# Seven products for the second group's down projection of a hybrid decoder layer

## The chip, the core and the metric

The kernel runs on one core of a Trainium2 chip. The core has TensorE (PE, matrix products), VectorE (DVE), ScalarE (ACT), GpSimd (POOL) and SyncE (SP), which here only issues transfers. The metric is the time of one execution in microseconds on the device; a kernel's time is the median of several timed runs. One more execution is taken with the profiler.

## The reference

One decoder layer is computed in fp32 for 2048 prompt tokens (16 blocks of 128) and 32 sample tokens, model width 1024, hidden width 4096:

```python
def decoder_layer(x, p, lp, state):
    xn = rms_norm(x, lp['norm_mix_pre'])
    qk_raw, v_m, o_m, gates, q_a, k_a, v_a = split_projection(xn @ lp['w_in'])
    ...
    mix = jnp.concatenate([y_m, y_a], axis=-1) @ lp['w_out']
    x = x + rms_norm(mix, lp['norm_mix_post'])
    u = rms_norm(x, lp['norm_ffn_pre'])
    f = jnp.square(jax.nn.relu(u @ lp['w_up'])) @ lp['w_down']
    x = x + rms_norm(f, lp['norm_ffn_post'])
    x = x + jax.nn.sigmoid(x @ lp['w_pgate']) * (p @ lp['w_pproj'])
    return x, (c_new, n_new, m_new, conv_new, k_new, v_new)
```

`y_m` is an mLSTM with four heads (chunks of 128 tokens), `y_a` a sliding-window attention with eight heads, both from the one projection. The change touches the product with `w_down`.

## The kernel before, in words

The blocks form six chunks (3, 3, 3, 3, 2, 2 blocks) and three groups of two chunks. First the projection with both attentions runs over all chunks (0 to about 700 us). Then each group goes through the output projection ("mix"), the MLP and the gate. The second group, whose MLP runs from about 1530 to 1960 us, is group 1 (blocks 6 to 11); the first group's MLP runs from 850 to 1300 us.

Every fp32 product is three passes on numbers that are split into a high and a low part, high x high, high x low and low x high (`mm3`). A high part is a cast on ScalarE, a low part a subtraction on VectorE or GpSimd (`split`, `wsplit`; L230 and L231 for hidden activations, L253 and L254 for weights). Weights come through a ring of 7 pair tiles (high and low, 512 KB) and 5 raw tiles. At its first use a weight tile is loaded raw, split, and stored to memory by GpSimd's queue (L281); later it is loaded already split by SP's queue (`w<-wk`).

The MLP goes through the hidden width in 16 steps of 256. In a step `up_both` makes the hidden activations of both chunks, each as two tiles of 128 x 384, by a Strassen scheme: seven products of four inner blocks each instead of eight (steps 2 to 15). Its sums are adds on VectorE that read PSUM (L1732), each followed by relu and square on ScalarE (L1652, L1653), a cast (L230) and a low part (L231). `down` then multiplies the hidden tiles with `w_down` plainly: 2 chunks x 2 halves of 512 columns x 3 blocks x 2 tiles x 3 passes, 72 matmuls of 128 x 512 a step. Each block and half ends in a PSUM buffer (three of them) that VectorE adds into `f` (L1757).

What sets the order: TensorE's work is written in program order. A class `Flow` counts TensorE's modelled time, and lets side generators (attention, sums of activations) emit their instructions when their due time, given by the numbers that they yield, is reached. A scheduler orders the other engines, except for instructions that are pinned in program order (`here`).

## Time and profile before

| what | us |
|---|---|
| median of three timed runs | 2620.46 (2619.96 to 2620.51) |
| the profiled execution | 2614.14 |
| its span in the trace | 2612.0 |
| TensorE busy in the span | 2525.7 |
| VectorE busy | 1481.4 |
| ScalarE busy | 973.9 |
| GpSimd busy | 620.4 |

The mean granted TensorE clock was 0.993. Times in the trace are counted from the start of the span. In rows of groups the two numbers behind the bar are the busy time of the group and the mean of one in ns; in rows of the timeline the first two are start and duration in us. "w" is a split weight, "wr" and "wb" a raw one, "wk" its stored copy, "hh" and "hl" the high and low part of hidden activations, "re" their sums before the split, "up" and "dn" the products in PSUM.

### The profile page before, as it was taken

The numbers are of one execution on the slowest core, as the hardware profiler recorded it, in microseconds if no ns is written. First come the engines' busy times: TensorE is split into PE (matmuls) and PEld (weight loads), VectorE is DVE, ScalarE is ACT, GpSimd is POOL, SyncE is SP. The second block draws the span as 40 slices with busy tenths as digits, with TensorE's granted clock in tenths as the row PEclk, the third lists the DMA queues.
The fourth block names the chain that finished last, engine by engine and source line by source line (L and its number), as shares of the span: only waits on it lengthen the run. The fifth ranks groups of instructions, "written<-read, shape, count | busy, mean of one in ns | idle before, by whom it ended". The sixth has DMA issues, their size and how long they took to land.

```text
span 2612.0 us, 39335 instructions
## 1 busy us (share of the span) xinstructions
PE 2525.7 (97%) x14260; PEld 2198.5 (84%) x14260; DVE 1481.4 (57%) x3162; ACT 973.9 (37%) x2167; POOL 620.4 (24%) x988
## 2 busy tenths in 40 slices
PE   7999999999899999999999999999999999999998
PEld 7788878878688888888877789999998879999986
DVE  6676666665667656656744654444446346545553
ACT  5545444444445444444523442222223134222232
POOL 5311111112433666666523300000001011000010
PEclk9999999999999999999999999999999999999999
DMA  9755656576798666666799765555556899777786
GB/s 321 280 201 182 216 176 221 202 254 217 253 345 291 256 248 254 243 254 250 268 344 316 262 208 185 193 186 188 188 189 231 296 332 360 257 254 254 256 304 236
DMA packets 220433, 651.10 MB, mean 249 GB/s; under 512 B 25397, under 2 KB 59401, under 8 KB 220224
## 3 DMA queue, kind: packets, MB, share of 16 engines
q1 hardware_dynamic: 170032, 474.02, 53.1%
q0 software_dynamic: 50160, 174.54, 17.3%
q8 instruction: 113, 1.85, 0.3%
q14 instruction: 80, 0.66, 0.1%
q10 hardware_dynamic: 48, 0.03, 0.0%
HBM read 494.34 MB, written 155.25 MB: 249 GB/s over the span
## 4 chain that ended last, share of the span: by engine, by line
PE 77%; DMA 8%; DVE 8%; issue 4%; ACT 3%; POOL 1%; SPq 0%; ACTq 0%; DVEq 0%; POOLq 0%
PE up L147 22%; PE dn L147 22%; PE pg L147 5%; PE mo L147 4%; PE v L147 3%; DMA w<-wk 3%; PE o L147 2%; DMA wk<-w 2%; PE qk L147 2%; PE gv L147 2%; DVE hl L231 1%; PE qa L147 1%; PE aT L151 1%; PE aO L147 1%; PE pv L147 1%
## 5 line engine op out<-in xcount | busy, mean ns | idle before, releaser
L147 PE MATMUL dn<-w,hh 128*128 128x512 f32 x1792 | 563.6, 396 | 7.2 <-ACT re L1652 4.2
L1757 DVE TENSOR_TENSOR f<-f,dn 128x512 f32<-128x512 f32 x420 | 287.2, 687 | 220.5 <-PE dn L147 218.4
L147 PEld LDWEIGHTS dn<-w,hh 128*128 128x128 f32 x1792 | 334.0, 189 | 85.5 <-DVE f L1757 7.0
L147 PE MATMUL dn<-w,hl 128*128 128x512 f32 x896 | 354.4, 396 | 1.6 <-DVE hl L231 1.6
L1732 DVE TENSOR_TENSOR re<-up,re 128x384 f32<-128x384 f32 (+1 forms) x294 | 152.0, 517 | 320.7 <-PE up L147 320.6
L147 PEld LDWEIGHTS dn<-w,hl 128*128 128x128 f32 x896 | 168.7, 188 | 43.3 <-DVE hl L231 5.2
L1733 ACT COPY re<-up 128x384 f32<-128x384 f32 (+1 forms) x42 | 18.8, 448 | 392.0 <-PE up L147 392.0
L1652 ACT ACTIVATE re<-re 128x384 f32<-128x384 f32 (+1 forms) x168 | 83.0, 494 | 206.7 <-DVE re L1732 203.2
L231 DVE TENSOR_TENSOR hl<-re,hh 128x384 fp32r<-128x384 f32 (+1 forms) x192 | 136.9, 713 | 16.1 <-ACT hh L230 15.1
L281 POOL DMA_DIRECT2D wk<-w x242 | 133.8, 556 | 30.0 <-DVE w L254 25.1
L253 ACT CAST w<-wr 128x512 fp32r<-128x512 f32 (+2 forms) x152 | 89.2, 597 | 94.6 <-PE up L147 31.1
L253 ACT CAST w<-wb 128x512 fp32r<-128x512 f32 x98 | 60.6, 620 | 168.5 <-PE dn L147 114.5
L254 POOL TENSOR_TENSOR w<-wr,w 128x512 fp32r<-128x512 f32 (+2 forms) x76 | 100.3, 1319 | 78.7 <-ACT w L253 77.7
L1459 POOL DMA_DIRECT2D x<-x1d x16 | 8.7, 545 | 463.5 <-PE up L147 449.4
L254 POOL TENSOR_TENSOR w<-wb,w 128x512 fp32r<-128x512 f32 x70 | 92.4, 1320 | 110.4 <-ACT w L253 110.0
L1653 ACT ACTIVATE re<-re 128x384 f32<-128x384 f32 (+1 forms) x192 | 94.9, 494 | 5.9
L230 ACT CAST hh<-re 128x384 fp32r<-128x384 f32 (+1 forms) x192 | 92.6, 482 | 8.3
L1066 ACT ACTIVATE s<-s,swt 128x257 f32<-128x257 f32 (+1 forms) x128 | 63.3, 496 | 66.1 <-DVE swt L1063 66.1
L1060 DVE CUSTOM_DVE_ANT_0 s<-aS,cst,sink 128x256 f32<-128x256 f32 (+1 forms) x128 | 57.1, 473 | 50.2 <-PE aS L147 49.8
L147 PE MATMUL up<-t2h,w 128*128 128x384 f32 (+1 forms) x336 | 85.2, 321 | 0.0
L147 PE MATMUL up<-t0h,w 128*128 128x384 f32 (+1 forms) x336 | 85.2, 320 | 0.0
L147 PE MATMUL up<-t1h,w 128*128 128x384 f32 (+1 forms) x336 | 85.1, 320 | 0.0
(1526 smaller groups left out, 6404.2 us busy)
## 6 DMA issues: line engine op xcount, KB each, us to landing
w<-wk SPq DMA_DIRECT2D x728, 512.0 KB, 4.7
wk<-w POOLq DMA_DIRECT2D x238, 512.0 KB, 7.5
wr<-in_w_down_dram SPq DMA_DIRECT2D x64, 256.0 KB, 8.2
wb<-in_w_up_dram SPq DMA_DIRECT2D x28, 512.0 KB, 6.8
w<-wk SPq DMA_DIRECT2D x20, 528.0 KB, 4.0
x<-in_x_prompt_dram SPq DMA_DIRECT2D x16, 512.0 KB, 4.6
y<-yd SPq DMA_DIRECT2D x32, 256.0 KB, 6.7
xr<-in_x_prompt_dram POOLq DMA_DIRECT2D x16, 512.0 KB, 8.6
```

Source lines behind the costliest of these rows:

```text
L147: ins = self.pe.matmul(out, lhsT, rhs, start=start, stop=stop)
L230: act.copy(hi, src)
L231: dve.tensor_tensor(lo, src, hi.bitcast(F32), ALU.subtract)
L253: act.copy(hi, src)
L254: ins = (eng or weng()).tensor_tensor(lo, src, hi.bitcast(F32), ALU.subtract)
L281: here(put(self.kept[key], t.bitcast(U32)))
L1060: dve.tensor_tensor_reduce(s_[:, s, lo : 2 * P], pS[:, s, lo:], bias[:, j, lo:], 1.0 if s == 0 else 0.0625, sink[:, h : h + 1], ALU.add, A ...
L1066: act.activation(e_, e_, AF.Exp, bias=nm[:, s : s + 1], accum_out=sm[:, s : s + 1])
L1652: act.activation(t, src, AF.Relu)
L1653: act.square(t, t)
L1732: add = lambda out, a, b: dve.tensor_tensor(out, a, b, ALU.add)
L1757: dve.tensor_tensor(out(i), out(i), ps, ALU.add)
```

## The change

In group 1, steps 2 to 13 (`SEVEN`, 12 steps) make the down product by seven products too. Two steps form a pair: `up_seven` makes the hidden tiles of each step and four more combinations of them (s1 to s4), and `down_seven`, after the odd step, runs seven products, each over the two steps in one PSUM buffer. A product is added into one or two halves of `f`, or into an accumulator U of three tiles, which `share` adds to three quarters of `f` after step 13. Of the sums, s1, t1 and t3 (the inputs of s2 and s4) and the low parts of s1, s2 and s4 are on GpSimd.

The right sides are three plain blocks of `w_down` a step and four differences of blocks. The differences are made in the projection: a new side generator, `differences`, starts with the second chunk. For each step it loads four blocks on GpSimd's queue into raw tiles of the ring, subtracts four times on GpSimd and stores four tiles (`td`). In the MLP they are loaded raw by SP's queue and split, cast on ScalarE and low part on GpSimd. The tile pools are shared out anew: the ring's `wide` pool is closed at step 2 in group 1, `sp2` has one buffer, the gain for the norm after the MLP is loaded behind `share` in this group. `MIXF` lets the preparation of the second chunk's mix in group 0 start later behind its loads (18 instead of 6).

```diff
--- before
+++ changed
...
 MIXW = 6.0
+MIXF = 18.0
 LODVE = 2
 STEPS = FF // (FS * P)
+SEVEN = range(2, STEPS - 2)
+SGROUP = 1
+DIFW = 10.0, 4.0, 10.0
...
             return self.get(key, n, make)
+        def diff(self, key, src):
+            def make(h, l):
+                raw = self.load(512)
+                dma(raw, src)
+                wsplit(h, l, raw, pool)
+            return self.get(key, 512, make)
...
             return ("u", s, q), lambda key: ring.multi(key, [(0, FS * P, rows)], 2, FS * P)
+        def diff(s, i):
+            return ("t", s, i), lambda key: ring.diff(key, td[s, i])
+        def rows_seven(steps):
+            for i, k, half in ((0, 0, 0), (3, 0, 0), (0, 1, 0), (1, 0, 0), (4, 0, 0), (0, 1, 1), (2, 0, 0)):
+                for s in steps:
+                    yield diff(s, i) if i else row(w_down, s * FS + k, half)
...
                     yield product(s, i)
-                yield from rows_down(s)
+                if gi == SGROUP and s in SEVEN:
+                    if s % 2:
+                        yield from rows_seven((s - 1, s))
+                else:
+                    yield from rows_down(s)
...
+    td = {(s, i): dram.tile([P, 512], F32, name=f"td{s}{i}") for s in SEVEN for i in range(1, 5)}
     ring.set_plan(plan())
+    def differences():
+        sub = lambda out, a, b: here(pool.tensor_tensor(out, a, b, ALU.subtract))
+        for s in SEVEN:
+            b11, b21, b12, b22 = b = [ring.load(512) for _ in range(4)]
+            for n, t in enumerate(b):
+                k = s * FS + n % 2
+                here(put(t, w_down[k * P : (k + 1) * P, n // 2 * 512 : n // 2 * 512 + 512]))
+            yield DIFW[0]
+            for i, out, x, y in ((1, b11, b12, b11), (3, b12, b22, b12), (2, b22, b22, b11), (4, b21, b21, b22)):
+                sub(out, x, y)
+                yield DIFW[1]
+            for i, out in ((1, b11), (3, b12), (2, b22), (4, b21)):
+                here(put(td[s, i], out))
+            yield DIFW[2]
...
     for ci, blocks in enumerate(CHUNKS):
+        if ci == 1:
+            prep.add(differences())
         project(ci, blocks)
     pe.drain(swa)
+    pe.drain(prep)
...
             todo.append((None, "s", load_y(lp, "ld", "s")))
-        yield MIXW
+        yield MIXF if (gi, ci) == (0, 1) else MIXW
...
     wp = es2.enter_context(tc.tile_pool(name="wp", bufs=WBUF, reuse_waits="tile"))
-    sp2 = es2.enter_context(tc.tile_pool(name="sp2", bufs=2, reuse_waits="tile"))
+    sp2 = es2.enter_context(tc.tile_pool(name="sp2", bufs=1, reuse_waits="tile"))
     open_lp()
     dec = pe.side()
     def mlp(gi, chunks, sample):
         nonlocal gffn
-        gffn = gain(A["norm_ffn_post"], f"gffn{gi}")
         G = f"{gi}"
+        if gi != SGROUP:
+            gffn = gain(A["norm_ffn_post"], f"gffn{gi}")
...
                         pool.tensor_copy(y[:, W : W + HS], hid["s", ft, e])
+        def rectify(t):
+            act.activation(t, t, AF.Relu)
+            act.square(t, t)
+        def parts(pool_, t, nm, eng):
+            h, l = [pool_.tile([P, UW], F32R, tag=f"h{e}", name=f"h{e}{nm}")[:, : t.shape[1]] for e in "hl"]
+            act.copy(h, t)
+            eng.tensor_tensor(l, t, h.bitcast(F32), ALU.subtract)
+            return h, l
+        def up_seven(s, X, hq, wq):
+            W = X[0][0].shape[2]
+            nm = f"{G}{s}"
+            product = products(s, X)
+            A = {}
+            t = [wp.tile([P, UW], F32, tag="re", name=f"re{nm}{n}")[:, :W] for n in range(4)]
+            s1 = wq.tile([P, UW], F32, tag="s1", name=f"s1{nm}")[:, :W]
+            add = lambda out, a, b: dve.tensor_tensor(out, a, b, ALU.add)
+            act.copy(t[0], product(1))
+            add(t[1], product(2), t[0])
+            rectify(t[1])
+            A["11"] = parts(hp, t[1], f"{nm}a11", dve)
+            add(t[0], product(6), t[0])
+            add(t[2], product(7), t[0])
+            add(t[3], product(4), t[2])
+            rectify(t[3])
+            A["12"] = parts(hp, t[3], f"{nm}a12", dve)
+            ps = product(5)
+            add(t[2], ps, t[2])
+            add(t[0], ps, t[0])
+            rectify(t[2])
+            A["22"] = parts(hp, t[2], f"{nm}a22", dve)
+            add(t[0], product(3), t[0])
+            rectify(t[0])
+            pool.tensor_tensor(s1, t[0], t[2], ALU.add)
+            dve.tensor_tensor(t[0], t[1], t[0], ALU.subtract)
+            A["s3"] = parts(hq, t[0], f"{nm}s3", dve)
+            A["s1"] = parts(hq, s1, f"{nm}s1", pool)
+            pool.tensor_tensor(t[1], s1, t[1], ALU.subtract)
+            pool.tensor_tensor(t[3], t[3], t[1], ALU.subtract)
+            A["s4"] = parts(hq, t[3], f"{nm}s4", pool)
+            A["s2"] = parts(hp if s % 2 else hq, t[1], f"{nm}s2", pool)
+            return A
+        def down_seven(s, As, U, first):
+            c0, c1 = chunks
+            def out(ci, half):
+                return lambda i: f[chunks[ci][i]][:, half * 512 : half * 512 + 512]
+            u = lambda i: U[i]
+            uses = (
+                ("11", u, out(0, 0)),
+                ("s3", out(1, 1), out(1, 0)),
+                ("12", out(0, 0)),
+                ("s1", out(1, 1), out(0, 1)),
+                ("22", out(1, 0)),
+                ("s4", out(0, 1)),
+                ("s2", u),
+            )
+            for n, (a, *to) in enumerate(uses):
+                w = [[t[:, :512] for t in w] for w in ring.take(2)]
+                for i in range(len(c0)):
+                    ps = psum(ps_mm, f"ds{G}{s}{n}{i}")
+                    for e in range(2):
+                        mm3(ps, [y[:, cols(i)] for y in As[e][a]], w[e], e == 0, e == 1)
+                        pe.tick()
+                    for m, o in enumerate(to):
+                        if first and n == 0 and m == 0:
+                            act.copy(o(i), ps)
+                        else:
+                            dve.tensor_tensor(o(i), o(i), ps, ALU.add)
+        def share(U):
+            for ci, half in ((0, 1), (1, 0), (1, 1)):
+                for i, b in enumerate(chunks[ci]):
+                    v = f[b][:, half * 512 : half * 512 + 512]
+                    pool.tensor_tensor(v, v, U[i], ALU.add)
...
                 tp = es_t.enter_context(tc.tile_pool(name="tp", bufs=1, side="right", reuse_waits="tile"))
-                ring.wide = es_t.enter_context(tc.tile_pool(name="wide", bufs=WIDE, side="right", reuse_waits="tile"))
+                es_w = ExitStack()
+                ring.wide = es_w.enter_context(tc.tile_pool(name="wide", bufs=WIDE, side="right", reuse_waits="tile"))
...
         for s in range(FAST, STEPS):
+            if gi == SGROUP and s in SEVEN:
+                if s == SEVEN[0]:
+                    es_w.close()
+                    es_w = ExitStack()
+                    side = lambda nm, n: es_w.enter_context(tc.tile_pool(name=nm, bufs=n, side="right", reuse_waits="tile"))
+                    hq, wq = side("hq", 5), side("wq", 1)
+                    U = gp.tile([P, 2, 512], F32, tag="g", name=f"us{G}")
+                    U = [U[:, 0], U[:, 1], side("us", 1).tile([P, 512], F32, name=f"ut{G}")]
+                    As = []
+                As.append(up_seven(s, X, hq, wq))
+                if len(As) == 2:
+                    down_seven(s, As, U, s == SEVEN[1])
+                    As = []
+                if s == SEVEN[-1]:
+                    share(U)
+                    gffn = gain(A["norm_ffn_post"], f"gffn{gi}")
+                continue
             hid = {}
             up_both(s, X, hid)
             if s == STEPS - 1:
+                es_w.close()
...
```

Three places show how instructions move. The first is VectorE in group 1 where step 7's `up` ends and the down product begins. Before, from the last add on `up` (`hl17..` are low parts of step 7's hidden tiles, `dn17..` its down products, `f6` to `f11` the outputs):

```order
L1732 TENSOR_TENSOR re170_17187<-up173_17306,re170_17187 128x384
L231 TENSOR_TENSOR hl1711_17303<-re172_17189,hh1711_17302 128x384
L1757 TENSOR_TENSOR f6_14249<-f6_14249,dn1706_17336 128x512
L231 TENSOR_TENSOR hl1710_17325<-re170_17187,hh1710_17324 128x384
L1757 TENSOR_TENSOR f7_14250<-f7_14250,dn1707_17344 128x512
L1757 TENSOR_TENSOR f8_14251<-f8_14251,dn1708_17352 128x512
L1757 TENSOR_TENSOR f6_14249<-f6_14249,dn1716_17360 128x512
L1757 TENSOR_TENSOR f7_14250<-f7_14250,dn1717_17368 128x512
```

With the change (`ds17..` are the pair's products, n and block in the last two digits; `us1`, `ut1` are U; `re170<-re171,re170` is the subtraction for s3):

```order
L1731 TENSOR_TENSOR re170_17460<-up173_17580,re170_17460 128x384
L1787 TENSOR_TENSOR us1_16207<-us1_16207,ds1700_17622 128x512
L1787 TENSOR_TENSOR f6_14489<-f6_14489,ds1700_17622 128x512
L1749 TENSOR_TENSOR re170_17460<-re171_17461,re170_17460 128x384
L1787 TENSOR_TENSOR us1_16207<-us1_16207,ds1701_17631 128x512
L1720 TENSOR_TENSOR hl17a22_17577<-re172_17462,hh17a22_17576 128x384
L1720 TENSOR_TENSOR hl17s3_17601<-re170_17460,hh17s3_17600 128x384
L1787 TENSOR_TENSOR f7_14490<-f7_14490,ds1701_17631 128x512
L1787 TENSOR_TENSOR ut1_16211<-ut1_16211,ds1702_17640 128x512
L1787 TENSOR_TENSOR f8_14491<-f8_14491,ds1702_17640 128x512
L1787 TENSOR_TENSOR f9_14849<-f9_14849,ds1710_17659 128x512 x2
```

The low parts of a22 and s3 now stand behind three adds of the first product and one subtraction that reads two tiles of SBUF. On GpSimd the program before has nothing at this place; with the change (`w611` and on are low parts of td tiles, `s117`, `re171` and `re173` the sums):

```order
L258 TENSOR_TENSOR w615_17714<-wr615_17715,w615_17714 128x512
L1748 TENSOR_TENSOR s117_17464<-re170_17460,re172_17462 128x384
L1752 TENSOR_TENSOR re171_17461<-s117_17464,re171_17461 128x384
L1753 TENSOR_TENSOR re173_17463<-re173_17463,re171_17461 128x384
L1720 TENSOR_TENSOR hl17s2_17615<-re171_17461,hh17s2_17614 128x384
L258 TENSOR_TENSOR w616_17719<-wr616_17720,w616_17719 128x512
L258 TENSOR_TENSOR w617_17751<-wr617_17752,w617_17751 128x512
L1720 TENSOR_TENSOR hl17s1_17605<-s117_17464,hh17s1_17604 128x384
L258 TENSOR_TENSOR w618_17756<-wr618_17757,w618_17756 128x512
L1720 TENSOR_TENSOR hl17s4_17611<-re173_17463,hh17s4_17610 128x384
```

GpSimd's sums and low parts of activations are mixed with low parts of weights. The second place is GpSimd in the projection, around blocks 3 to 5. Before:

```order
L973 DMA yd30_108<-ym3_2948 128x512
L1056 COPY s61_3396<-sink_101 128x2
L945 TENSOR_TENSOR m4f_3142<-m4f_3142,nhalf_92 128x4
L973 DMA yd40_110<-ym4_3141 128x512
L1056 COPY s62_3479<-sink_101 128x2
L1099 DMA yd51_113<-ya5_3079 128x512
L1111 TENSOR_TENSOR rsa_96<-swt5_2646,nhalf_92 128x1
L945 TENSOR_TENSOR m5f_3176<-m5f_3176,nhalf_92 128x4
L973 DMA yd50_112<-ym5_3175 128x512
```

With the change (`wr76` are raw tiles with blocks of `w_down`, `td5.` the stored differences of step 5):

```order
L1141 DMA yd51_161<-ya5_3183 128x512
L496 TENSOR_TENSOR wr76_3074<-wr76_3076,wr76_3074 128x512
L496 TENSOR_TENSOR wr76_3076<-wr76_3077,wr76_3076 128x512
L1153 TENSOR_TENSOR rsa_144<-swt5_2736,nhalf_140 128x1
L987 TENSOR_TENSOR m5f_3282<-m5f_3282,nhalf_140 128x4
L1015 DMA yd50_160<-ym5_3281 128x512
L496 TENSOR_TENSOR wr76_3077<-wr76_3077,wr76_3074 128x512
L496 TENSOR_TENSOR wr76_3075<-wr76_3075,wr76_3077 128x512
L507 DMA td51_93<-wr76_3074 128x512
L507 DMA td53_95<-wr76_3076 128x512
L507 DMA td52_94<-wr76_3077 128x512
L507 DMA td54_96<-wr76_3075 128x512
```

Between the small steps of the attention (`rsa`, `m4f`, `m5f`) there are now four subtractions of 128 x 512 and four stores for a step. The third place is SP's queue. Before, the raw loads of `w_out` stand in the first part of the projection:

```order
L350 DMA wr218_7683<-in_w_out_dram 128x512
L350 DMA wr219_7752<-in_w_out_dram 128x512
L350 DMA wr220_7759<-in_w_out_dram 128x512
L288 DMA w37_1497<-wk0_193 128x1056
L288 DMA w38_1500<-wk1_200 128x1056
L288 DMA w39_1503<-wk2_208 128x1056
```

With the change they stand at its end, in front of loads of kept weights, and reuse raw tiles that held differences:

```order
L292 DMA w200_7278<-wk19_846 128x1024
L292 DMA w201_7461<-wk20_955 128x1024
L292 DMA w202_7472<-wk21_999 128x1024
L292 DMA w203_7519<-wk22_1015 128x1024
L354 DMA wr217_7917<-in_w_out_dram 128x512
L292 DMA w204_7529<-wk23_1031 128x1024
L292 DMA w205_7584<-wk24_1088 128x1024
L292 DMA w206_7620<-wk25_1110 128x1024
L292 DMA w207_7630<-wk26_1157 128x1024
L292 DMA w208_7651<-wk27_1179 128x1024
L292 DMA w209_7688<-wk28_1210 128x1024
L292 DMA w210_7717<-wk29_1270 128x1024
```

The rows behind `wr217` on this queue come after it has been issued.

More of the change, by code (lines that the diff above doesn't have):

```diff
@@ new lines, in share, with products, product @@
+        def share(U):
[3 more added lines that the diff above has]
+                    pool.tensor_tensor(v, v, U[i], ALU.add)
+        def products(s, X):
+            turn = iter(X)
+            def product(n):
+                ps = psum(ps_s, f"up{G}{s}{n}")[:, : X[0][0].shape[2]]
+                w, x = ring.take()[0], next(turn)
+                for k in range(4):
+                    mm3(ps, [t[:, k] for t in w], [t[:, k] for t in x], k == 0, k == 3)
+                    pe.tick()
+                return ps
+            return product
@@ L1720, in up_both @@
             nm = f"{G}{s}"
-            turn = iter(X)
-            def product(n):
-                ps = psum(ps_s, f"up{nm}{n}")[:, :W]
-                w, x = ring.take()[0], next(turn)
-                for k in range(4):
-                    mm3(ps, [t[:, k] for t in w], [t[:, k] for t in x], k == 0, k == 3)
-                    pe.tick()
-                return ps
+            product = products(s, X)
             t = [wp.tile([P, UW], F32, tag="re", name=f"re{nm}{n}")[:, :W] for n in range(4)]
```

2 lines of the change are left out of this document (1 added, 1 removed).

## The prediction

> **What bounds the kernel now.** I read the page's first and fourth parts first: busy shares, and the chain of work that ended last.
>
> ```profile
> PE 2525.7 (97%) x14260; PEld 2198.5 (84%) x14260; DVE 1481.4 (57%) x3162; ACT 973.9 (37%) x2167; POOL 620.4 (24%) x988
> PE 77%; DMA 8%; DVE 8%; issue 4%; ACT 3%; POOL 1%; SPq 0%; ACTq 0%; DVEq 0%; POOLq 0%
> ```
>
> TensorE is busy 97% of the span. A matmul taken away is worth its whole time, provided that nothing makes TensorE wait instead. The change works in two stages, so next I read the table of busy time by stretch (sum first, then each engine's busy time and count, granted clock, DMA share, GB/s):
>
> ```profile
> core 0: us, PE busy (x) PEld busy (x) DVE busy (x) ACT busy (x) POOL busy (x), PEclk, DMA share, GB/s
> 100.00:600.00 500.00, 481.98 (x3347) 413.37 (x3346) 323.71 (x1031) 242.40 (x647) 74.60 (x179) 1.00 0.64 217
> 850.00:1300.00 450.00, 444.63 (x2189) 392.35 (x2188) 279.41 (x407) 193.93 (x364) 280.85 (x311) 1.00 0.66 253
> 1300.00:1420.00 120.00, 114.96 (x525) 91.76 (x523) 57.15 (x117) 33.86 (x63) 35.99 (x60) 1.00 0.95 332
> 1530.00:1960.00 430.00, 429.71 (x2160) 388.34 (x2160) 205.15 (x327) 105.42 (x203) 1.12 (x2) 1.00 0.57 191
> ```
>
> 1530 to 1960 is the second group's MLP: TensorE never stops, VectorE is busy 48%, ScalarE 25%, GpSimd not at all. 100 to 600 is the projection: TensorE idles 18 us of 500, VectorE is at 65%, GpSimd at 15%. 850 to 1300 is the first group's MLP: the same matmuls, with GpSimd at 62% because weights are split there.
>
> **What is removed.** The timeline of TensorE gives a step of group 1, from the last `up` product to the next step's:
>
> ```profile
> 1599.01 0.34 PE L147 MATMUL up<-ut10h,w 128*128 128x384 f32 x1
> 1613.51 0.34 PE L147 MATMUL up<-ut11h,w 128*128 128x384 f32 x1
> 1613.68 0.63 PE L147 MATMUL dn<-w,hh 128*128 128x512 f32 x2
> 1629.99 0.40 PE L147 MATMUL dn<-w,hl 128*128 128x512 f32 x1
> 1630.22 0.34 PE L147 MATMUL up<-ut10h,w 128*128 128x384 f32 x1
> ```
>
> The down product runs from 1613.68 to 1630.22: 16.54 us for 72 matmuls, 0.2297 us each; the whole step is 31.2 us. Seven products for two steps are 7 x 3 blocks x 2 tiles x 3 passes = 126 matmuls in place of 144. Over six pairs 108 matmuls go: **-24.8 us**, if TensorE stays as dense as here.
>
> **What is added in group 1, off the path.** Prices:
>
> ```profile
> L1757 DVE TENSOR_TENSOR f<-f,dn 128x512 f32<-128x512 f32 x420 | 287.2, 687 | 220.5 <-PE dn L147 218.4
> L253 ACT CAST w<-wb 128x512 fp32r<-128x512 f32 x98 | 60.6, 620 | 168.5 <-PE dn L147 114.5
> L254 POOL TENSOR_TENSOR w<-wb,w 128x512 fp32r<-128x512 f32 x70 | 92.4, 1320 | 110.4 <-ACT w L253 110.0
> L254 POOL TENSOR_TENSOR w<-wr,w 128x256 fp32r<-128x256 f32 x8 | 6.3, 790 | 8.5 <-ACT w L253 8.4
> ```
>
> A pair (some 58 us) has 30 adds into f and U where it had 24 (+4.1 us on VectorE), 8 casts of td tiles (+5.0 us on ScalarE), and on GpSimd 8 splits of 1.3 us and, per step, 3 sums and 3 low parts of 384 columns. A 384-wide GpSimd operation is not in the trace; between 0.79 (256 wide) and 1.32 (512) I take 1.03. GpSimd then works 10.5 + 12.4 = 23 of 58 us, VectorE and ScalarE stay near half and a third. Throughput hides all of it; the cover is the matmuls of the pair. Weights grow from 8 x 512 KB to 6 x 512 + 8 x 256 KB a pair, at a DMA share of 0.57: nothing. What can cost is latency at one place.
>
> **The turn from the odd step's up to the pair's down.** Let T be the start of the first `ds` matmul. The second product reads the odd step's s3, and the order lists behind each other on VectorE: the last add of `re170`, two adds of ds1700, the subtraction for s3, an add of ds1701, the low part of a22, the low part of s3. ds1700 is 6 matmuls, ready at T+1.4. TensorE asks for s3's low part after 18 + 5 matmuls: T+5.28. Durations on the other engines are from the groups of 1550 to 1950:
>
> ```profile
> L1732 DVE TENSOR_TENSOR re<-up,re 128x384 f32<-128x384 f32 x85 | 47.3, 557 | 118.5 <-PE up L147 118.5
> L1652 ACT ACTIVATE re<-re 128x384 f32<-128x384 f32 x49 | 25.7, 525 | 95.9 <-DVE re L1732 95.9
> L230 ACT CAST hh<-re 128x384 fp32r<-128x384 f32 x50 | 25.7, 513 | 1.6
> L231 DVE TENSOR_TENSOR hl<-re,hh 128x384 fp32r<-128x384 f32 x49 | 27.0, 551 | 2.1 <-ACT hh L230 2.0
> ```
>
> The add ends at T+0.76; relu and square on ScalarE end at T+1.94; the adds of ds1700 hold VectorE to T+2.9. GpSimd meanwhile makes one weight split and s1 (to T+3.19). Then VectorE and GpSimd meet: both read two tiles of SBUF. The first group shows what that does. There the same low part (L231) takes 1275 ns, not 551:
>
> ```profile
> L231 DVE TENSOR_TENSOR hl<-re,hh 128x384 fp32r<-128x384 f32 x51 | 65.0, 1275 | 0.6 <-ACT hh L230 0.6
> 1014.03 2.62 DVE L231 TENSOR_TENSOR hl<-re,hh 128x384 fp32r<-128x384 f32 x1
> 1013.66 1.31 POOL L313 TENSOR_TENSOR wb<-wb 128x512 f32<-128x512 f32 x1
> 1014.93 1.29 POOL L312 TENSOR_TENSOR wb<-wb,wb 128x512 f32<-128x512 f32 x1
> 985.47 1.29 POOL L312 TENSOR_TENSOR wb<-wb,wb 128x512 f32<-128x512 f32 x1 [1.82 <-DMA wb<-in_w_up_dram]
> 985.53 1.64 DVE L231 TENSOR_TENSOR hl<-re,hh 128x384 fp32r<-128x384 f32 x1
> 986.72 1.61 POOL L319 TENSOR_TENSOR wb<-wb,wb 128x512 f32<-128x512 f32 x1
> ```
>
> At 1014.03 VectorE waits through two back-to-back GpSimd operations and ends 0.4 us after the second. At 985.53 it gets in after the first: the second, L319, needs the result of its predecessor, and starts late (1.61 instead of 1.29). So GpSimd keeps the tiles' access as long as its next operation is ready. Adds that read PSUM (L1757) show no such delay.
>
> In the pair's chain this gives: subtraction for s3 from T+3.22 to 3.77, t1 on GpSimd 3.8 to 4.82, ScalarE's copy of s3 4.2 to 4.7. The low part of a22 waits from 4.32 and gets in at 4.82, since the next GpSimd operation (t3) needs t1; it ends at 5.24, and s3's low part at 5.65. TensorE waits 0.4 us there and about 0.4 again for f7, queued behind it, to free a PSUM buffer: 0.85 us a pair. The first pair copies into U on ScalarE and has another order; I give it 2. Together **+6 us**. From odd to even steps I find 0.5 us of slack and no wait. If GpSimd instead holds on through t3, the low part of s2 and two weight splits, to T+9.9, s3's low part ends at T+10.3: 5.0 us a pair, 4 to 5 in the first, 30 in all. I take the low end since the dependent successor is the row of 985.53; both stay for the range.
>
> The Trainium skill ("SBUF — State Buffer", on who interferes with whom) states a narrower lock: whoever of the two starts first has the port pair for that instruction, and the other waits that long. By it the low part of a22 waits only for t1, the 30 us case is gone and the sum is the low one. The first group's rows agree on which operations collide, but the wait of 2.62 us over two instructions is more than the page says, so I keep the case.
>
> **share(U).** Nine GpSimd adds of 1.3 us, 11.7 us, run while the next step's `up` (14.7 us) covers them; they collide with its low parts: **+1 us**, at most 3. The gain load behind them is needed only at the last step.
>
> **What is added in the projection.** 48 subtractions of 1.30 us (62 us) and 96 DMA issues on GpSimd, with 25 MB:
>
> ```profile
> L281 POOL DMA_DIRECT2D wk<-w x242 | 133.8, 556 | 30.0 <-DVE w L254 25.1
> wr<-in_w_down_dram SPq DMA_DIRECT2D x64, 256.0 KB, 8.2
> 165.31 1.02 POOL L945 TENSOR_TENSOR m2f<-m2f,nhalf 128x4 f32<-128x4 f32 x1 [2.08 <-DVE m2f L944]
> 166.35 0.16 DVE L946 TENSOR_TENSOR m2f<-m2f 128x4 f32<-128x4 f32 x1 [0.80 <-POOL m2f L945]
> ```
>
> The issues are 96 x 0.556 = 53 us, so GpSimd goes from 75 to about 190 of 500. 25 MB over some 430 us add 58 GB/s to 217, a share of about 0.8; the stretch 1300 to 1420 ran at 0.95 with TensorE busy 96%. So transfers cost little. Two things cost: VectorE is held up, and small GpSimd steps on the way to VectorE (L945 above, ahead of the block's output) queue behind subtractions. For the first, the two MLPs are the measure: in group 0, 51 low parts lose 0.72 us each, 37 us in all, and its step lasts longer. Eleven steps lie between these two rows:
>
> ```profile
> 905.34 0.33 PE L147 MATMUL up<-ut00h,w 128*128 128x384 f32 x1
> 1256.61 0.34 PE L147 MATMUL up<-ut00h,w 128*128 128x384 f32 x1
> ```
>
> That is 31.93 us a step against 31.21 in group 1, 0.72 us more, 9 us over the 13 steps of the 51 low parts: about a quarter of VectorE's loss reaches TensorE. In the projection 62 us of subtractions meet a VectorE at 65%, with part of its rows from PSUM: 20 to 40 us lost, 5 to 10 on TensorE; I take 6 for both things together.
>
> The handoff comes next. The differences take four of the ring's five raw tiles until the last td store has landed, after the projection. In before the first w_out rows are loaded at 98 us; now they, and SP's queue behind them, wait for those stores. That load, the stretch of the handoff in the table, and the chain there:
>
> ```profile
> 98.37 13.28 SPq L350 DMA_DIRECT2D wr<-in_w_out_dram  x4
> 660.00:720.00 60.00, 53.42 (x267) 41.01 (x266) 40.28 (x83) 27.04 (x62) 27.64 (x36) 0.94 0.80 253
> 655.91 0.48 PE spo L147 x2
> 659.21 5.66 DMA y<-yd
> 668.81 1.30 POOL w L254
> 670.12 3.81 DMA wr<-in_w_out_dram
> 713.95 11.61 DMA w<-wk
> ```
>
> A raw load is 3.8 us and four splits on GpSimd 5.2; the chain has a raw load already. Between 0 and 8 us, I take 4. Together **+10 us**, from 3 to 25 (62 us all lost on VectorE / 4 = 16, and 8, rounded up). MIXF starts the preparation of group 0's second mix chunk later behind its loads; I cost it at 0, and if it comes late, the 8 us cover it.
>
> **Sum.** -24.8 + 6 + 1 + 10 = -7.8 us against the profiled execution's 2614.1: 2606.3. That execution is 6.3 us under the median of the timed runs, 2620.5, so the forecast is 2612.7, told as **2612 us**. A measurement of this kernel can tell about 0.2%, 5.2 us, from no change.
>
> **Rivals.**
> - *The projection hides the differences.* GpSimd has 425 of 500 us free there, and the handoff falls into TensorE's own waits of 6.6 us between 660 and 720. Against: VectorE at 65% and the L945 row. Then -24.8 + 6 + 1 + 1 = -17: 2603.
> - *GpSimd holds VectorE off at the turn.* The order puts GpSimd operations that may be ready one behind another, from T+4.8 to 9.9, in the stretch where s3's low part is due. For it: 1014.03. Against: 985.53. Then -24.8 + 30 + 1 + 10 = +16: 2636. It makes the kernel slower as soon as the wait exceeds (24.8 - 1 - 10) / 6 = 2.3 us a pair.
> - *The projection takes the gain.* Its upper end, 25 us, from subtractions that hold small steps of every block: -24.8 + 6 + 1 + 25 = +7: 2627; in milder form no change.
> - *TensorE is not shortened*, because the twelve steps still issue as many matmuls: the order has 108 fewer, so I give it nothing.
>
> **How the numbers follow.** Forecast 0.52, projection hidden 0.15, hold at the turn 0.17, projection takes the gain 0.16. The forecast's own range is 2605 to 2619. Of its chance 0.42 lies below 2615.2, the rest is no change; the second is faster; the third is slower but for 0.02; the fourth is slower 0.09, no change 0.07. That makes faster 0.57, same 0.19, slower 0.24. The range that holds 8 in 10 is 2600 to 2634.
>
> **What would show it.** In the second group's MLP, of 430 us, about 18 us less (-24.8 + 7), with TensorE's idle time near 7 us and gaps under 1.5 us ahead of the second product of each pair; gaps of 5 us there, released by the low part of s3, show the third case. VectorE's low parts in the odd steps last 0.9 to 1.3 us, not 0.55. The projection ends 3 to 10 us later, its L231-like rows longer. The stretch to the first w_out product is up to 8 us longer, its chain through a td store and a w_out load. Wrong would be: TensorE gaps elsewhere in the pair (a late td split), or a per-matmul time other than 0.23 us.

## The result

The changed kernel takes 2638.64 us (median of four runs, 2636.28 to 2645.99) beside 2620.49 us of the kernel before: a ratio of 1.0081, 95% interval 1.0066 to 1.0096. It is slower by 0.8%; 2612 had been forecast. The profiled execution took 2636.28 us, the shortest of the four. Ratios here and below leave out two single executions that took 12 and 17% longer at a granted clock of 0.80 and 0.75.

The two rows of the page that were read first, after the change (busy shares; the chain that ended last):

```profile
PE 2517.0 (96%) x14152; PEld 2185.0 (83%) x14152; DVE 1547.5 (59%) x3207; ACT 1016.2 (39%) x2254; POOL 881.3 (33%) x1261
PE 70%; DVE 10%; DMA 9%; issue 3%; POOL 3%; ACT 3%; SPq 0%; ACTq 0%; POOLq 0%; DVEq 0%
```

The 108 matmuls are gone, but TensorE's busy time fell by only 8.7 us, and its share of the chain from 77% to 70%. Five marks from TensorE's timeline tell where the time went: the first product of the second chunk, the first product of the sixth chunk, the first `up` of the first group's MLP, and the first `up` of steps 2 and 14 in the second group. Before:

```profile
134.73 0.39 PE L147 MATMUL gv<-w,x1h 128*128 128x264 f32 x1
569.15 0.36 PE L147 MATMUL gv<-w,x5h 128*128 128x264 f32 x1
764.84 0.35 PE L147 MATMUL up<-ut00h,w 128*128 128x384 f32 x1
1567.47 0.35 PE L147 MATMUL up<-ut10h,w 128*128 128x384 f32 x1
1943.71 0.33 PE L147 MATMUL up<-ut10h,w 128*128 128x384 f32 x1
```

After:

```profile
139.75 0.51 PE L151 MATMUL gv<-w,x1h 128*128 128x264 f32 x2
601.31 0.48 PE L151 MATMUL gv<-w,x5h 128*128 128x264 f32 x2
797.19 0.35 PE L151 MATMUL up<-ut00h,w 128*128 128x384 f32 x1
1603.61 0.35 PE L151 MATMUL up<-ut10h,w 128*128 128x384 f32 x1
1964.12 0.34 PE L151 MATMUL up<-ut10h,w 128*128 128x384 f32 x1
```

The marks also show that the first group's MLP begins at 765 us and the second's at 1480: the stretches 850 to 1300 and 1530 to 1960 named ahead of the prediction are parts of them.

- First chunk: 5.0 us later. Other kernels below have this mark between 134.4 and 139.3, with and without differences; it is not put down to the change.
- Chunks 2 to 5: 461.6 instead of 434.4 us, **+27.1**.
- Sixth chunk, handoff and first output projection: 195.9 instead of 195.7, +0.2.
- First group's MLP to step 2 of the second: 806.4 instead of 802.6, +3.8.
- The twelve steps: 360.5 instead of 376.2, **-15.7**.
- From step 14 to the end of the span (2634.5 against 2612.0): +2.1.

So the second group does about what was forecast, and the projection costs far more. The table of busy time has the same two stretches as before:

```profile
100.00:600.00 500.00, 463.66 (x3084) 394.00 (x3082) 332.93 (x975) 226.74 (x609) 166.75 (x293) 0.98 0.71 244
1530.00:1960.00 430.00, 423.75 (x2122) 375.53 (x2121) 244.39 (x399) 160.44 (x316) 138.89 (x122) 1.00 0.63 207
```

In the projection TensorE now idles 36 us of 500 where it idled 18, and its granted clock is 0.98 instead of 1.00. What TensorE waited for in chunks 2 to 5, after the change (total us, times, longest):

```profile
PE aT L155 <- DVE s L1112: 14.4, 8, 4.7
```

and the first of these before:

```profile
PE aT L151 <- DVE s L1070: 1.3, 3, 0.5
```

`s` are the softmax weights of the window attention, and `aT` their transposition. The longest wait shows the cause. TensorE's row, then GpSimd and VectorE some 12 us before the wait begins:

```profile
431.98 0.45 PE L155 MATMUL aT<-ident,s 128*128 128x128 f32 x1 [4.68 <-DVE s L1112]
```

```profile
416.09 5.62 POOL L496 TENSOR_TENSOR wr<-wr,wr 128x512 f32<-128x512 f32 x4
```

```profile
415.79 1.88 DVE L933 TENSOR_TENSOR_SCAN R<-R,zero 4x128 f32<-4x128 f32 x1
417.71 1.48 DVE L934 TENSOR_TENSOR R<-R 4x384 f32<-4x384 f32 x1
419.22 1.40 DVE L938 TENSOR_TENSOR_SCAN Mt<-R,mp 4x128 f32<-4x128 f32 x1
420.65 1.07 DVE L939 TENSOR_TENSOR mp<-R,Mt 4x1 f32<-4x1 f32 x1
```

The four rows of VectorE are steps of the mLSTM's running maximum, each of which needs the one before. Before the change they took 0.41, 0.55, 0.47 and 0.15 us (groups of the same chunks, below). Now each of them lasts until one of GpSimd's four subtractions has ended, 4.3 us more in all (1.88 + 1.48 + 1.40 + 1.07 - 1.58). The chain of waits leads from here over ScalarE's exponentials to the softmax at 431.5, and TensorE stands for 4.68 us. A wait of 2.83 us ahead of 307.76 leads over the same steps.

```profile
L891 DVE TENSOR_TENSOR_SCAN R<-R,zero 4x128 f32<-4x128 f32 x11 | 4.4, 406 | 0.1
L892 DVE TENSOR_TENSOR R<-R 4x384 f32<-4x384 f32 x3 | 1.6, 546 | 0.1
L896 DVE TENSOR_TENSOR_SCAN Mt<-R,mp 4x128 f32<-4x128 f32 x11 | 5.1, 467 | 0.2
L897 DVE TENSOR_TENSOR mp<-R,Mt 4x1 f32<-4x1 f32 x11 | 1.6, 147 | 0.3
```

A second, rarer way in which GpSimd delays VectorE is its queue: a small copy stood behind a subtraction that waited for its block of `w_down`, and VectorE 6.4 us for the copy, once. TensorE's wait of 3.88 us ahead of 459.06 leads back to it.

```profile
451.86 1.29 POOL L496 TENSOR_TENSOR wr<-wr,wr 128x512 f32<-128x512 f32 x1 [5.65 <-DMA wr<-in_w_down_dram]
455.40 0.17 DVE L807 COPY u<-hist 128x3 f32<-128x3 f32 x1 [6.44 <-POOL hist L809]
```

In the second group the turn from the odd step's `up` to the pair's product is where the prediction had it. TensorE stops at the second product's first low part of step 7; VectorE's low part of s3 is held by GpSimd's t3 (L1753):

```profile
1757.29 0.39 PE L151 MATMUL ds<-w,hh17s 128*128 128x512 f32 x1
1759.01 0.49 PE L151 MATMUL ds<-w,hl17s 128*128 128x512 f32 x1 [1.09 <-DVE hl17s L1720]
1757.61 1.35 DVE L1720 TENSOR_TENSOR hl17s<-re,hh17s 128x384 fp32r<-128x384 f32 x1
1757.35 1.20 POOL L1753 TENSOR_TENSOR re<-re,re 128x384 f32<-128x384 f32 x1
```

The gap is 1.09 us, the same in five of the six pairs. The next block's first matmul then starts at 1759.61, 0.60 us later instead of 0.23: in the six pairs weight loads wait 2.8 us in all, seven times, for VectorE's adds into `f`, which free the PSUM buffers.

### The profile page after: what moved, and what is told of

Its sections match the earlier page's. It is cut to its first block, busy times and chain, and to the rows that moved or that the text cites. A ratio compares the mean times of both kernels' runs of the same rounds, so it can differ in the third digit from the quotient of the medians.

```text
span 2634.5 us, 39839 instructions
## 1 busy us (share of the span) xinstructions
PE 2517.0 (96%) x14152; PEld 2185.0 (83%) x14152; DVE 1547.5 (59%) x3207; ACT 1016.2 (39%) x2254; POOL 881.3 (33%) x1261
## 4 chain that ended last, share of the span: by engine, by line
PE 70%; DVE 10%; DMA 9%; issue 3%; POOL 3%; ACT 3%; SPq 0%; ACTq 0%; POOLq 0%; DVEq 0%
PE up L151 20%; PE dn L151 13%; PE ds L151 6%; PE pg L151 5%; PE mo L151 5%; DMA w<-wk 4%; DMA wk<-w 3%; PE v L151 3%; PE o L151 2%; DVE hl L235 2%; PE qa L151 1%; PE pv L151 1%; POOL w L258 1%; PE gv L151 1%; PE aT L155 1%
## 5 line engine op out<-in xcount | busy, mean ns | idle before, releaser
L151 PE MATMUL dn<-w,hh 128*128 128x512 f32 x1216 | 383.7, 397 | 6.8 <-ACT re L1699 4.1
L151 PEld LDWEIGHTS dn<-w,hh 128*128 128x128 f32 x1216 | 225.7, 188 | 61.2 <-DVE f L1892 7.5
L1892 DVE TENSOR_TENSOR f<-f,dn 128x512 f32<-128x512 f32 x276 | 188.0, 685 | 131.6 <-PE dn L151 129.4
L151 PE MATMUL dn<-w,hl 128*128 128x512 f32 x608 | 240.9, 396 | 1.5 <-DVE hl L235 1.5
L1867 DVE TENSOR_TENSOR re<-up,re 128x384 f32<-128x384 f32 (+1 forms) x210 | 105.2, 501 | 203.7 <-PE up L151 203.6
L258 POOL TENSOR_TENSOR w<-wr,w 128x512 fp32r<-128x512 f32 (+2 forms) x124 | 161.9, 1310 | 130.5 <-ACT w L257 129.4
L285 POOL DMA_DIRECT2D wk<-w x242 | 134.4, 558 | 30.3 <-DVE w L258 24.0
L151 PEld LDWEIGHTS dn<-w,hl 128*128 128x128 f32 x608 | 114.6, 188 | 31.3 <-DVE hl L235 5.4
L1787 DVE TENSOR_TENSOR f<-f,ds 128x512 f32<-128x512 f32 x144 | 93.4, 681 | 33.9 <-PE ds L151 32.0
L1699 ACT ACTIVATE re<-re 128x384 f32<-128x384 f32 (+1 forms) x120 | 57.8, 482 | 112.9 <-DVE re L1867 109.6
L1731 DVE TENSOR_TENSOR re<-up,re 128x384 f32<-128x384 f32 x84 | 46.6, 555 | 80.1 <-PE up L151 80.1
```

Of the source, the lines that this page charges most:

```text
L151: ins = self.pe.matmul(out, lhsT, rhs, start=start, stop=stop)
L258: ins = (eng or weng()).tensor_tensor(lo, src, hi.bitcast(F32), ALU.subtract)
L285: here(put(self.kept[key], t.bitcast(U32)))
L1699: act.activation(t, src, AF.Relu)
L1731: add = lambda out, a, b: dve.tensor_tensor(out, a, b, ALU.add)
L1787: dve.tensor_tensor(o(i), o(i), ps, ALU.add)
```

## The experiments

All times below are medians beside runs of the kernel before on the same chip (2617.2 to 2617.7 us there). Beside that, the changed kernel's ratio of 1.0081 would be about 2639.

### Taking the two places apart

**Without the differences in the projection.** The second group reads plain blocks of `w_down` in their place.

```diff
-    td = {(s, i): dram.tile([P, 512], F32, name=f"td{s}{i}") for s in SEVEN for i in range(1, 5)}
+    blk = lambda k, h: w_down[k * P : (k + 1) * P, h * 512 : h * 512 + 512]
+    td = {(s, i): blk(s * FS + i % 2, i // 3) for s in SEVEN for i in range(1, 5)}
...
-        if ci == 1:
-            prep.add(differences())
```

> The changed kernel without the differences in the projection: no loads, subtractions or stores there; the second group loads plain blocks of w_down in place of the four differences (so the four differences are left out and the down product of these 12 steps is another one; all instructions of the second group stay). Theory 1 (the projection takes the gain, 32 us, and the second group gives 15.7): 2638.6 - 32 = about 2606, within 4. Theory 2 (the seven products do not pay, or the moved tile pools cost elsewhere): 2620 or more.

2600.12 us, ratio 0.9932 (0.9916 to 0.9948). The seven products pay: -17.6 us. What the differences take is about 39 us beside this kernel by the medians, where 32 had been expected, and 32.6 by the spans of the two profiled executions (2634.5 and 2601.9). The second number is lower because one is the shortest of its four executions and the other the longest.

**The differences alone**, with the plain down product in all steps.

```diff
-                if gi == SGROUP and s in SEVEN:
-                    if s % 2:
-                        yield from rows_seven((s - 1, s))
-                else:
-                    yield from rows_down(s)
+                yield from rows_down(s)
...
-        if gi != SGROUP:
+        if True:
...
-            if gi == SGROUP and s in SEVEN:
+            if False:
```

> The changed kernel with the plain down product in all steps, but with the differences still made and stored in the projection (nothing reads them). Theory 1: the projection's cost stands alone, 2620.5 + 32 = about 2652, within 5. Theory 2: at most 2630.

2650.74 us, ratio 1.0128 (1.0109 to 1.0148): +33 us, as expected. The cost stands without the second group's change; that it is 33 here and 39 above is within the scatter of these medians.

### What in the differences costs

**Without the subtractions**, loads and stores kept.

```diff
-                sub(out, x, y)
```

> The changed kernel without the 48 subtractions in the projection: blocks of w_down are loaded and stored as they are (the differences are left out), loads and stores on GpSimd's queue stay. If the subtractions cost by holding VectorE off (62 us of GpSimd, some 24 us longer VectorE instructions seen), 15 to 25 us of the 32 go: 2614 to 2624. If GpSimd's queue, which waits for loads and stores to land and keeps small copies behind it, is the cause, or the 25 MB of traffic, less than 10 us go: 2629 to 2638.

2609.72 us, ratio 0.9969 (0.9956 to 0.9983): 9.6 us above the kernel without differences. The subtractions carry 29 of about 39 us, more than either theory's number; loads, stores and queue the rest. In chunks 2 to 5 loads and stores lengthen TensorE's stretch by 4.2 us and VectorE's busy time by 0.4. Without differences, then with loads and stores alone:

```profile
138.10:573.12 435.02, 420.43 (x2870) 360.34 (x2869) 282.27 (x909) 208.38 (x557) 54.59 (x138) 1.00 0.62 204
138.25:577.49 439.24, 423.66 (x2871) 362.93 (x2869) 282.72 (x909) 208.29 (x557) 95.11 (x218) 0.99 0.72 250
```

**The subtractions alone**, with blocks loaded and stored once.

```diff
-            return ("t", s, i), lambda key: ring.diff(key, td[s, i])
+            return ("t", s, i), lambda key: ring.diff(key, td[i])
...
-            b11, b21, b12, b22 = b = [ring.load(512) for _ in range(4)]
-            for n, t in enumerate(b):
+            if s == SEVEN[0]:
+                b11, b21, b12, b22 = b = [ring.load(512) for _ in range(4)]
+            for n, t in enumerate(b if s == SEVEN[0] else ()):
...
-                here(put(td[s, i], out))
+                if s == SEVEN[0]:
+                    here(put(td[i], out))
```

> The changed kernel with the 48 subtractions in the projection, but the four blocks are loaded and four tiles stored once instead of twelve times (the other steps reuse them, so the differences are not those of their steps). If the subtractions hold VectorE off: 2630 to 2638. If queue waits or traffic are the cause: 2606 to 2616.

2630.57 us, ratio 1.0046 (1.0028 to 1.0064): 30.5 us above the kernel without differences. The two parts (9.6 and 30.5) add up to the whole within 2 us. GpSimd's queue has nothing to wait for here, and VectorE's waits for results of GpSimd in chunks 2 to 5 add up to 18.2 us against 17.7 without subtractions. What is left is that VectorE's instructions themselves last longer (311.5 us busy in this stretch).

**Write instead of read.** Each subtraction is replaced by two fills of the same tile.

```diff
-                sub(out, x, y)
+                here(pool.memset(out, 0.0))
+                here(pool.memset(out, 0.0))
```

> The changed kernel with each subtraction of the projection replaced by two fills of the same tile with zero on GpSimd: it works in the same places and waits for the same loads, but reads nothing (the differences are left out). If VectorE is held off by GpSimd's reads (the port theory): about what loads and stores alone cost, 0.996 to 0.999 of before, and VectorE's instructions in the projection as long as before. If GpSimd's time on its queue, or its writes, cause the cost: 1.003 or more.

2612.35 us, ratio 0.9981 (0.9971 to 0.9990), 2.6 us above the kernel with loads and stores alone. In chunks 2 to 5 GpSimd fills for 46 us where the subtractions took 57.5, and waits as long for the loads. But the scan of the running maximum lasts 467 ns as before the change, where it lasts 551 beside subtractions. The groups of the fills and the scan, and of the changed kernel's subtractions and scan:

```profile
L504 POOL MEMSET wr<- 128x512 f32 x43 | 23.7, 551 | 20.3 <-DMA wr<-in_w_down_dram 20.3
L505 POOL MEMSET wr<- 128x512 f32 x43 | 22.6, 529 | 1.8
L939 DVE TENSOR_TENSOR_SCAN Mt<-R,mp 4x128 f32<-4x128 f32 x11 | 5.1, 467 | 0.2
```

```profile
L496 POOL TENSOR_TENSOR wr<-wr,wr 128x512 f32<-128x512 f32 x43 | 57.5, 1336 | 23.3 <-DMA wr<-in_w_down_dram 22.1
L938 DVE TENSOR_TENSOR_SCAN Mt<-R,mp 4x128 f32<-4x128 f32 x11 | 6.1, 551 | 0.2
```

So most of the hold comes with GpSimd's reads, not with its time or its queue. Not all of it: VectorE is busy 288.0 us in chunks 2 to 5 beside the fills, against 282.7 with loads and stores alone and 309.9 beside subtractions. The 5 us are mostly in VectorE's instructions with one input tile, such as small copies (beside fills, then before the change):

```profile
L808 DVE COPY u<-hist 128x3 f32<-128x3 f32 x16 | 4.5, 281 | 4.0 <-POOL hist L810 2.8
L765 DVE COPY u<-hist 128x3 f32<-128x3 f32 x16 | 2.7, 169 | 1.4
```

The Trainium skill ("SBUF — State Buffer", on who interferes with whom) says that a VectorE instruction with two SBUF inputs contends with a GpSimd instruction that reads SBUF and not with one that only writes; the scan, which has two inputs, agrees.

**On VectorE itself.** Loads and stores stay on GpSimd's queue.

```diff
-        sub = lambda out, a, b: here(pool.tensor_tensor(out, a, b, ALU.subtract))
+        sub = lambda out, a, b: here(dve.tensor_tensor(out, a, b, ALU.subtract))
```

> The changed kernel with the 48 subtractions of the projection on VectorE instead of GpSimd (about 0.69 us each, 33 us; loads and stores stay on GpSimd's queue). Theory V: any time that VectorE loses in the projection reaches TensorE nearly whole, since VectorE's steps there are a chain that TensorE waits for; then 33 us of own work cost about what the 28 us of longer instructions cost, 20 to 30 us: 1.003 to 1.010 of before. Theory Q: the cost comes from GpSimd's side (its small steps behind subtractions, or single VectorE steps held off at a bad moment); then it falls to what loads and stores alone cost, 0.996 to 1.000 of before.

2616.72 us, ratio 0.9996 (0.9986 to 1.0006). Theory V falls: 33 us of VectorE's own work cost 7 us over loads and stores, while 28 us of held instructions cost some 29. Theory Q's range holds: the cost comes from GpSimd's side, and of its two causes the runs above leave the held instructions, not the queue. The stretch of chunks 2 to 5 shows both (sum, then busy time of TensorE, its weight loads, VectorE, ScalarE and GpSimd, clock, DMA share, GB/s), for the kernel before, the changed kernel and this one:

```profile
134.73:569.15 434.42, 420.41 (x2870) 360.55 (x2869) 282.30 (x909) 208.31 (x557) 54.22 (x138) 1.00 0.61 206
```

```profile
139.75:601.31 461.56, 429.56 (x2870) 367.00 (x2869) 309.89 (x909) 206.98 (x557) 151.20 (x261) 0.98 0.70 238
```

```profile
137.26:581.58 444.32, 423.73 (x2871) 361.98 (x2869) 305.85 (x950) 208.52 (x557) 96.41 (x218) 0.99 0.72 248
```

VectorE is busy 24 to 28 us longer in both, but TensorE's stretch grows by 27 us in the one and by 10 in the other. A likely reason, which no run isolates, is that the scheduler knows of a subtraction on VectorE and orders it between chains, while a hold from another engine falls on whatever runs.

### Where else the differences could be made

**The same on VectorE, paced faster** (steps of 24 us in the order's time instead of 36, so that they end at about the start of the fifth chunk, and in a second kernel `DIFW = 8.0, 2.0, 2.0`, which makes 18 us, not the 16 of its expectation).

```diff
-DIFW = 10.0, 4.0, 10.0
+DIFW = 10.0, 2.0, 6.0
```

> Subtractions on VectorE as in the run at 0.9996, but paced faster, 24 instead of 36 us of the order's time a step, so that the last difference is stored before the fifth chunk, where kept weights already keep the DMA at 1.0. What loads and stores cost there (3 to 6 us in the fifth chunk and some at the output projection) should go: 0.995 to 0.998. If the pace only moves the cost to earlier chunks: 0.999 to 1.001.

> The same with 16 us a step: blocks are subtracted 8 us after their loads were issued. If loads have landed by then, like the run at 24 us, 0.995 to 0.998; if VectorE has to wait for them at the head of its queue: 1.000 to 1.006.

2615.70 us, ratio 0.9992 (0.9981 to 1.0004), and 2614.95 us, 0.9991 (0.9980 to 1.0002): no gain over 2616.72. The fifth chunk shrinks from 92.9 to 86.8 us in both, but chunks 2 to 4 grow by 10 and 13.

**In the second group, from raw blocks when they are due** (two to four loads for each difference, nothing stored).

```diff
...
-                raw = self.load(512)
-                dma(raw, src)
+                raw, *rest = [self.load(512) for _ in src]
+                for t, v in zip((raw, *rest), src):
+                    dma(t, v)
+                for t, op in zip(rest, (ALU.subtract, ALU.add, ALU.subtract)):
+                    here(pool.tensor_tensor(raw, raw, t, op))
                 wsplit(h, l, raw, pool)
...
```

> The changed kernel without stored differences: in the second group each difference is made when its weight is due, from 2 to 4 raw blocks of w_down (11 loads of 256 KB and 7 subtractions on GpSimd a step, where 4 loads were). Nothing in the projection or the first group. GpSimd goes to about 41 of 60 us a pair, DMA to about 0.8. If VectorE has slack outside the turn from up to down: 1 to 2 us a pair, 0.994 to 0.998. If the second group's pairs are near the edge: 5 us a pair, 1.004.

2717.15 us, ratio 1.0379 (1.0364 to 1.0395): a miss, 117 us above the kernel without differences. In the second group TensorE waits 78 us for late weights, each behind up to four loads into five raw tiles and their subtractions; the granted clock there is 0.88 where it was 1.00. Throughput is not short: from 1600 to 2000 us GpSimd is busy 205 of 400 us, and the DMA share is 0.60.

```profile
PE ds L151 <- ACT w L257: 62.3, 24, 4.8
PE ds L151 <- POOL w L258: 15.4, 24, 0.9
```

**In the first group's MLP**, where the four blocks are loaded anyway: one subtraction and one store after each quarter of a step's down product (`ring.raws` holds the step's four raw tiles, and each `next` subtracts and stores once).

```diff
...
             wd = [down_weights() for half in range(2)]
+            dif = differences(s, ring.raws) if gi == 0 and s in SEVEN else iter(())
             for ci in range(2):
                 for half in range(2):
                     down(s, ci, half, wd[half], hid)
+                    next(dif, None)
```

On GpSimd:

> The changed kernel with the differences made in the first group's MLP, on GpSimd, from the raw blocks of w_down that are loaded there anyway, one subtraction and one store after each quarter of a step's down product; nothing in the projection. Theory V (VectorE has slack in an MLP, a quarter of its loss reaches TensorE): 62 us of subtractions cost about 8 us there, 2600 + 8 beside 2617.7 of before: 0.995 to 0.998. If subtractions cost as much here as in the projection (30 us): 1.003 to 1.006.

2660.68 us, ratio 1.0164 (1.0148 to 1.0180): a miss by 50 us. GpSimd's other work there is preparing weights, and VectorE's part in that is held: its low parts of `up` weights take 2124 ns where they took 684. The adds into `f` queue behind, and TensorE waits for them. Over the whole first group VectorE is busy 56 us longer than in the kernel without differences, and TensorE's stretch is 60 us longer (that kernel's row last):

```profile
L258 DVE TENSOR_TENSOR w<-wb,w 128x512 fp32r<-128x512 f32 x28 | 59.5, 2124 | 5.5 <-ACT w L257 5.4
PE dn L151 <- DVE f L1885: 43.9, 19, 4.4
760.00:1355.00 595.00, 545.25 (x2591) 477.82 (x2590) 397.83 (x498) 238.51 (x448) 403.38 (x448) 0.95 0.69 254
762.80:1297.70 534.90, 524.84 (x2593) 464.54 (x2592) 341.78 (x498) 238.06 (x448) 314.96 (x352) 0.99 0.69 259
```

On VectorE:

> The same with the subtractions on VectorE (33 us on an engine that is busy 62% there, no meeting with GpSimd). Theory V: 0.994 to 0.998, a few us less than on GpSimd if holding is what costs, a few more if VectorE's own time is.

2624.26 us, ratio 1.0014 (1.0002 to 1.0026). Far better than on GpSimd, but TensorE now waits for sums of `up` that stand on VectorE behind late splits of the next down weights:

```profile
PE up L151 <- DVE re L1860: 20.5, 12, 2.8
```

**The same on VectorE, all four behind the first quarter.**

```diff
                     down(s, ci, half, wd[half], hid)
-                    next(dif, None)
+                    for _ in dif:
+                        pass
```

> The version with the differences in the first group's MLP on VectorE, but all four subtractions and stores right behind the first quarter of a step's down product. In the version with one after each quarter (1.0014) TensorE waited 20.5 us, in 12 waits, for sums on VectorE that stood behind late splits of the next down weights, whose raw tiles were freed late. If the late raw tiles are the cause, freeing them some 10 us earlier takes most of these waits away: 0.994 to 0.998. If the added work on VectorE is: still 1.000 or more.

2591.72 us, ratio **0.9914** (0.9899 to 0.9928): faster than both kernels. Against the one without any differences the ratio is lower by 0.0018, about 5 us, and the two intervals overlap; but the profiles show the first group's MLP in 524 us, against 535 there. The wait for `re` is gone, as expected if late raw tiles were its cause. The first group's step falls too, from 31.9 us before the change to 31.4. VectorE and GpSimd meet less there: the low part of a hidden tile takes 900 ns in the first group, where it took 1145 before the change (over the whole group; the first row is this kernel's, the second that of before).

```profile
L235 DVE TENSOR_TENSOR hl<-re,hh 128x384 fp32r<-128x384 f32 x64 | 57.6, 900 | 3.5 <-ACT hh L234 3.5
```

```profile
L231 DVE TENSOR_TENSOR hl<-re,hh 128x384 fp32r<-128x384 f32 x64 | 73.3, 1145 | 2.8 <-ACT hh L230 2.8
```

Why they meet less, and whether that is what shortens the step, was not tested.

## Why the prediction was wrong, point by point

- **Removed, -24.8 us: right** as a count (108 matmuls) and per matmul (the first six of the pair at 1752.40 take 1.40 us). The twelve steps gained 15.7 us where the sum had -24.8 + 6 = -18.8.
- **The turn, +6 us: right in mechanism, low in size.** The gap stands at the forecast instruction, the low part of s3, and VectorE got in between two GpSimd operations, so the third case (30 us, 2636) did not come about, though its time is near the measured one: right time, wrong mechanism. The gap is 1.09 us instead of 0.4, because GpSimd's t3 holds the low part of s3 itself (1.35 instead of 0.55 us), which the arithmetic let run free once a22 was through. The wait for a PSUM buffer behind it, put at about 0.4 us, is 0.4. (The arithmetic counted an add of ds1701 at 0.55 us where its row has 0.69; that moves nothing.) Over five pairs a pair takes 60.3 us, and 62.7 (376.2 / 6) - 18 x 0.2297 = 58.6 were ideal: 1.7 us instead of 0.85. The first pair, put at 2 us, took 59.0: 0.4.
- **share, +1 us: nearly nothing.** Step 14, the one over its adds, takes 31.5 us against 31.4 before.
- **The projection, +10 us, 3 to 25: the step that failed.** The forecast of VectorE's loss, 20 to 40 us, was right: 27.6 us (309.9 - 282.3). What failed is "about a quarter of VectorE's loss reaches TensorE". The quarter was taken from the first group's MLP, where VectorE's adds and splits are loosely tied to TensorE. In the projection the recurrence is a chain of short steps, each of which can be held for a whole subtraction (at 416 to 422 us four in a row were), and TensorE stood behind it. Its stretch grew by 27 us; 4 of these come with loads and stores alone, which leaves 22 us (461.6 - 439.2) for 27 us of held instructions: four fifths, not a quarter. Nor is the quarter a property of loosely tied work: with 48 more subtractions on GpSimd in the first group's MLP, 56 us more on VectorE cost 60. For VectorE's own time it would have done: the subtractions on VectorE added 23 us to its busy time in chunks 2 to 5 and 5 to the stretch (444.3 - 439.2). The upper end of 25 rested on the same quarter and fell with it.
- **The clock was not in the sum.** Of the 27 us in chunks 2 to 5, 18 are more idle time of TensorE (461.6 - 429.6 against 434.4 - 420.4), and 9 are longer busy time for the same 2870 matmuls, at a granted clock of 0.98. They go together: stretches of 20 us with a gap of 2.2 to 4.7 us show 0.91 to 0.97.
- **The handoff, +4 us, 0 to 8: about right, but hidden.** From the sixth chunk to the first group's `up` it is 195.9 us, as before the change (195.7), but 189.6 in the kernel without differences. The loss lies between the first product of the output projection and the first `up`; the rows are of the kernel before, the changed one and the one without differences:

```profile
673.96:764.84 90.88, 80.96 (x372) 63.33 (x371) 55.30 (x110) 39.41 (x89) 33.63 (x47) 0.94 0.83 285
706.18:797.19 91.01, 82.01 (x371) 64.13 (x370) 56.55 (x110) 39.28 (x89) 33.63 (x48) 0.92 0.85 287
678.64:762.68 84.04, 78.71 (x372) 60.98 (x370) 55.01 (x110) 39.26 (x89) 33.27 (x47) 0.98 0.87 309
```

In all five kernels that make no differences in the projection this stretch takes 83.7 to 86.3 us. So the differences cost some 6 us here, and something else in the change gives as much back. Whether that is `MIXF`, and whether the late loads of `w_out` are what costs, no run isolates.
- **Transfers at no cost: low.** Loads and stores alone cost 9.6 us (0.9969 against 0.9932): 4.2 in chunks 2 to 5, and 4.5 in the handoff (194.1 against 189.6), where the term for it counted them. Part of the first is in the fifth chunk (90.4 instead of 87.3 us), where kept weights alone already take the DMA to a share of 1.0 in one stretch of 20 us.
- **The chances.** "The projection takes the gain" had 0.16 and 2627; it was the right case with too small a price.

Two small things stay open. In the kernels with seven products the gate after the first group waits 2 to 3 us for a kept weight where it waited 0.7, and the third group is some 2 us longer; neither was tested. And the times of the changed kernels scatter over some 5 to 13 us, those of the kernel before over 1 us on the first chip but over 4 to 13 on the later ones.

## What to carry to other kernels

A hold of one engine by another must be priced at the chain it falls on, not by an average from another stage or another load: read off the first group's MLP, a quarter of it reached TensorE; under the projection's recurrence it was four fifths, and in that same MLP with 48 more subtractions all of it. Before GpSimd is chosen because it is idle, ask whether its operation reads two SBUF tiles beside VectorE's chains; here the same subtraction was cheaper on the busier VectorE. And where the operands of preparatory work are in SBUF anyway, do it there, early enough that their buffers are free for the next loads: that turned +0.8% into -0.9%.

## What was not expected of the hardware

- VectorE's short instructions were held one GpSimd operation each, the scan over 4 partitions as well (1.88 us instead of 0.41). At 416 to 421 us both engines took turns, while at 1014 us in the kernel before VectorE waited through two GpSimd operations. The prediction's reading that GpSimd keeps the access as long as its next operation is ready is therefore not general. When it is the one and when the other, these runs do not tell.
- A GpSimd fill of 128 x 512 took 0.55 and 0.53 us, and VectorE's scans beside it were not longer (467 ns); its copies of 128 x 3 were (281 instead of 169 ns).
- In chunks 2 to 5, 18 us more idle time of TensorE came with 9 us more busy time at a lower clock. That is no fixed rate: with loads and stores alone, 1.0 us more idle time came with 3.2 us (423.66 against 420.43). The Trainium skill ("TensorE: Matmul & The Clock Gate", on why this matters for your kernels) warns of gaps above about 3 us; here one of 2.8 us, ahead of 307.8, already goes with a granted clock of 0.91 in its stretch of 20 us (the row's third number from the end). The second row has no gap above 2.15 us, ahead of 587.68; in the kernel before, the same gap ahead of 556.54, and one of 3.03 us ahead of 130.07 (third row), left the clock at 1.00. The length of a gap alone does not decide.

```profile
300.00:320.00 20.00, 17.17 (x99) 16.40 (x99) 15.83 (x44) 9.19 (x20) 5.70 (x10) 0.91 0.77 275
580.00:600.00 20.00, 16.88 (x112) 12.90 (x109) 11.93 (x38) 10.45 (x29) 7.89 (x12) 0.91 0.67 227
120.00:140.00 20.00, 16.97 (x137) 14.27 (x136) 14.17 (x45) 10.10 (x26) 2.12 (x5) 1.00 0.78 266
```
